# Twenty-four modulation vectors of layer 0: products on VectorE or on TensorE

## The chip, the core and the metric

The kernel runs on one NeuronCore of one Trainium2 chip. A core has engines that run side by side, each with its own instruction stream in program order: TensorE (PE, matrix products; its weight loads are shown apart as PEld), VectorE (DVE), ScalarE (ACT), GpSimd (POOL) and SyncE (SP), which here only starts DMA transfers. They wait for each other on semaphores. Data lie in SBUF (128 partitions) and PSUM (eight banks of 128 x 512 fp32, where TensorE writes). The metric is device microseconds (us) of one execution.

## The reference, cut to what matters

One step of a two-layer backbone over 1152 tokens (1024 latent, 128 context) of width 1024, with three token mixers (latent attention, mLSTM, HGRN2), an output projection and a SwiGLU feed-forward part. Each layer begins with modulation: six vectors of 1024 numbers for each of two conditions (`c` and `c_ctx`).

```python
def trunk_layer(x, cvec, lp, lb, cache, rope):
    mod = (jax.nn.silu(cvec) @ lp['w_mod'] + lp['b_mod'])[:, None, :]
    sh1, sc1, g1, sh2, sc2, g2 = jnp.split(mod, 6, axis=-1)
    h = x * (1 + sc1) + sh1
    ... h @ lp['w_in'], the three mixers, mix = concat @ lp['w_out']
    x = layernorm(ALPHA * x + g1 * mix, ...)
    h2 = x * (1 + sc2) + sh2
    ... feed-forward
    x = layernorm(ALPHA * x + g2 * (...), ...)
```

`w_mod` is 1024 x 6144 for each layer. In slices of 128 columns that is 48 products a layer, numbered j = 0 to 47: j 0 to 7 are `sh1`, 8 to 15 `sc1`, 16 to 23 `g1`, 24 to 31 `sh2`, 32 to 39 `sc2`, 40 to 47 `g2`. `sh1` and `sc1` are needed at once; `g1`, `sh2`, `sc2` only after the mixers.

## The kernel before, in words

The program goes layer by layer through phases A (input projections, HGRN2, preparation of the attention, mLSTM), B (attention), C (output projection) and D (feed-forward). Most products are fp32 split into a high and a low fp32r half and done as three matmuls (L155, L156, L157 in `mm3`); some, such as the mLSTM's, are plain fp32 matmuls, which the trace shows as two records each.

The modulation vectors sit in `modfm`, a tile with the 128 columns of a slice on the partitions and (j, condition) along the free axis. Those of layer 0 are made at three places: j 0 to 15 in the start stage (`start`, j 8 to 15 on TensorE at L251), j 40 to 47 later, and **j 16 to 39 in the background of other work**, by a generator `bg` that `start_mod` makes. At each `next(bg)` it does one j: a 512 KB transfer of the slice (L211, a ring of two buffers `raw`), and for each condition one VectorE instruction (L213) that multiplies 128 x 1024 weights by the condition, broadcast beforehand to all partitions (`cB`, L127, two transfers of 512 KB in each place), and accumulates the row sums into one column of `modfm`. Every eighth j adds the bias (`mod_bias`, L220). After j 23, `gsave` transposes the finished `g1` (L225) and stores it.

The generator is called at two places:

- zone "gemv" in phase A, j 16 to 23: once for each token tile n of the `gi` projection (evacuation L399), then for each tile of `ckv` and `cq` in `mla_prep`. These are long runs of `mm3` matmuls in PSUM banks 0 to 2 (`r_mm`), whose results VectorE takes out. In the same stretch VectorE prepares the gates of HGRN2 (L528 to L537).
- the mLSTM's output, `mlstm`, j 24 to 39: twice for each of nine token tiles n. For each n the scores of four heads (L830, into banks 3 and 4, `r_a`), the decay mask and exponential on POOL and ACT, the product with the scores on VectorE (L839), the state's part (L845, 128 x 130) and the values' part (L850, 128 x 65, both into banks 5 to 7, `r_m`), evacuations on VectorE (L846, L853) and the norm. Rows `snr` (L825) and queries `smq` (L826) are loaded for each n.

The order of instructions on each engine is not that of the code: the program is built with `schedule_with_timeline_sim=True`, and a list scheduler with its own model places them. So work of the next stage (rotations and query products of the attention, L1104 and L1134) stands among that of the mLSTM, and a change in one stage can shift the order in others. Each engine then keeps its order strictly. SP's queue too is in order: a transfer whose buffer isn't free yet holds up those behind it.

Layer 1 runs the same stages without `bg` (all its 48 vectors are made elsewhere), which makes it a comparison.

Of the kernel before, what the change touches and what calls it, by code (L numbers as in the profile page):

```python
# [20 lines left out]
P = 128  # L21
D = 1024
# [75 lines left out]
class Builder:  # L98
# [60 lines left out]
    def setup(self):  # L159
        nc, ctx, ins = self.nc, self.ctx, self.ins  # L160
        self.pp = self.pool(ctx, "persist")
        self.dram = self.pool(ctx, "scratch", bass.MemoryType.DRAM)
        self.pps = self.pool(ctx, "psum", bass.MemoryType.PSUM)
        t = self.tile
        self.bank = [t(self.pps, [P, 512], F32, "bank") for _ in range(8)]
        self.ident = t(self.pp, [P, P], name="ident")
        make_identity(nc, self.ident)
        self.hhi = t(self.pp, [P, KD, T], F32R, "hhi")
        self.hlo = t(self.pp, [P, KD, T], F32R, "hlo")
        self.cols = t(self.pp, [P, DEPTH, NCOL], name="cols")  # L170
        nc.sync.dma_start(self.cols, ins["cols"])
        self.modfm = t(self.pp, [P, DEPTH, 48, 2], name="modfm")
        self.gates = t(self.pp, [P, NT, 16], name="gates")
        self.gT = t(self.pp, [16, P], name="gT")
        self.mhalf = t(self.pp, [P, 8], name="mhalf")
        nc.vector.memset(self.mhalf, -0.5)
        lbt = t(self.pp, [P, 12], name="lbt")
        lb0 = self.cols[:, 0, COL_OFF["lb"][0]:COL_OFF["lb"][0] + 4].rearrange("p (a d) -> p a d", d=2)
        L = lbt.rearrange("p (a b) -> p a b", b=6)
        nc.vector.tensor_tensor(L[:, :, 0:1], lb0[:, :, 0:1], lb0[:, :, 1:2], op=ALU.max)  # L180
        nc.vector.tensor_tensor(L[:, :, 1:3], lb0, L[:, :, 0:1].to_broadcast([P, 2, 2]), op=ALU.subtract)
        nc.scalar.activation(L[:, :, 1:3], L[:, :, 1:3], AF.Exp)
        nc.vector.tensor_tensor(L[:, :, 3:4], L[:, :, 1:2], L[:, :, 2:3], op=ALU.add)
        nc.vector.reciprocal(L[:, :, 3:4], L[:, :, 3:4])
        nc.vector.tensor_tensor(L[:, :, 1:3], L[:, :, 1:3], L[:, :, 3:4].to_broadcast([P, 2, 2]), op=ALU.mult)
        self.lbL = L
        dr = self.dram
        self.s_x = t(dr, [T, D], name="sx")
        self.s_x2 = t(dr, [T, D], name="sx2")
        self.s_tm = {k: t(dr, [T, 256], name="s" + k) for k in ("mo", "gg")}  # L190
        self.s_cq = t(dr, [P, 2, T], name="scq")
        self.s_ck = t(dr, [P, T], name="sck")
        self.s_kp = t(dr, [32, T], name="skp")
        self.s_mq = t(dr, [P, 2, T], name="smq")
        self.s_rec = t(dr, [T, 512], name="srec")
        self.s_c = t(dr, [2, D], name="scr")
        self.s_g = {g: t(dr, [16, P], name="sg") for g in (16, 40)}
        self.s_nr = t(dr, [8, T], name="snr")
        self.s_ri = [t(dr, [1, 512], name="sri") for _ in range(4)]
        self.s_dn = [t(dr, [1, 512], name="sdn") for _ in range(4)]  # L200
        self.s_ws = t(dr, [8, T], name="sws")
        self.s_ex = [t(dr, [P, 4, T2], name="sex") for _ in range(3)]
        self.s_h = [[t(dr, [NT, P, b - a, P], name="shid") for a, b in ps] for ps in PASSES]
# [31 lines left out]
    def start(self, z):  # L235
        nc, ins = self.nc, self.ins
        accs = [(i // NB, i % NB, self.bank[i]) for i in range(7)]
        cin, cc = z([P, KD, 2]), z([P, KD, 2])
        cB, junk = [z([P, D]), z([P, D])], z([P, D], BF16)
        rm, rx, rt = z.ring(6, [P, U]), z.ring(6, [P, T]), z.ring(2, [P, T])  # L240
        nc.sync.dma_start(cin, ins["cvec"])
        nc.scalar.activation(cc, cin, AF.Silu)
        bm = self.col(0, "bmod")
        xs, ws = [], []

        def mods(k):
            v, j = rm.next(), 8 + k
            nc.sync.dma_start(v, ins["w_mod"][0, j])
            ps = self.bank[7][:, 2 * j:2 * j + 2]
            for i in range(KD):  # L250
                nc.tensor.matmul(ps, v[:, i * P:(i + 1) * P], cc[:, i, :], start=(i == 0), stop=(i == KD - 1))  # L251
            nc.vector.tensor_scalar(self.modfm[:, 0, j, :], ps, bm[:, j:j + 1], 1.0, op0=ALU.add, op1=ALU.add)
            if k == 0:
                self.mod_init(cB, ins["crow"])
                for s in range(2):
                    nc.scalar.activation(cB[s], cB[s], AF.Silu)
                    nc.sync.dma_start(self.s_c[s:s + 1, :], cB[s][0:1, :])
            self.mod_gemv(0, k, cB, rm.next(), junk)
            self.mod_bias(0, k, 1)
            xs.append(rx.next())  # L260
            nc.sync.dma_start(xs[k], ins["xT"][:, k, :])

        mods(0)
        for k in range(KD):
            if k < 3:
                ws.append(self.unit(ins["w_in"][0, k]))
            if k + 1 < KD:
                mods(k + 1)
            x2 = rt.next()
            for s, c in ((0, slice(0, NLAT)), (1, slice(NLAT, T))):  # L270
                if s == 0:
                    nc.scalar.activation(x2[:, c], xs[k][:, c], AF.Identity, bias=self.modfm[:, 0, k, s:s + 1], scale=self.modfm[:, 0, 8 + k, s:s + 1])
                else:
                    nc.vector.tensor_scalar(x2[:, c], xs[k][:, c], self.modfm[:, 0, 8 + k, s:s + 1], self.modfm[:, 0, k, s:s + 1], op0=ALU.mult, op1=ALU.add)
            self.split(self.hhi[:, k, :], self.hlo[:, k, :], x2, nc.vector if k % 2 else nc.gpsimd)
            for u, b, ps in accs:
                if u < len(ws):
                    for kk in (range(k + 1) if u == k else (k,)):
                        self.fm_step(ps, ws[u], kk, b)
        return ws, accs  # L280

    def start_mod(self, z, j0, j1):
        raw = z.ring(2, [P, U])
        cB, junk = [z([P, D]), z([P, D])], z([P, D], BF16)
        self.mod_init(cB)

        def gen():
            for j in range(j0, j1):
                self.mod_gemv(0, j, cB, raw.next(), junk)
                if j % 8 == 7:  # L290
                    self.mod_bias(0, j - 7, 8)
                if j == 23:
                    self.gsave(0, 16, self.r_m.next())
                yield

        return gen()

# [69 lines left out]
    def phase_a(self, l):  # L367
# [5 lines left out]
        with ExitStack() as cA:  # L373
# [10 lines left out]
            with ExitStack() as cH:  # L384
# [4 lines left out]
                with ExitStack() as c0:  # L389
                    zs = Zone(self, c0, f"hs{l}", "right")  # L390
                    set0 = [zs([P, T]) for _ in range(5)]
                    self.mark(f"hg{l}")
                    g.project(0, set0, early if l == 0 else None)
                    self.row(l, "b_gi", br)
                    with ExitStack() as c:
                        bg = self.start_mod(Zone(self, c, "gemv"), 16, 24) if l == 0 else iter(())

                        def gi(ps, tt):
                            V.tensor_tensor(v[:, tt, :], ps, br, op=ALU.add)  # L399
                            next(bg, None)  # L400

                        self.win_tm(l, "gi", gi)
                        g.prep(0, set0, rW)
                        self.mark(f"mp{l}")
                        self.mla_prep(l, Zone(self, c, f"mp{l}"), bg, (brx, nr))
                    self.mark(f"hs{l}")
                    zt = Zone(self, cH, f"ht{l}")
                    set1 = [zt([P, T]) for _ in range(5)]
                    g.states(0, set0, v, rW)
                    for b in range(NB):  # L410
                        g.outs(0, b, set0, v, rW)
                        g.project_unit(1, b, set1)
# [28 lines left out]
            self.mark(f"ml{l}")  # L441
            with ExitStack() as c:
                zl = Zone(self, c, f"ml{l}")
                bg = self.start_mod(zl, 24, 40) if l == 0 else iter(())
                self.mlstm(l, gates, vaug, mkT, Cst, zl, bg)
                for i in tail:
                    fill[int(i)]()
# [1242 lines left out]
def pack(i):  # L1690
# [8 lines left out]
    a["w_mod"] = np.concatenate([  # L1699
        wm[0, :, :, :8].transpose(2, 3, 0, 1).reshape(8, P, 1024),  # L1700
        wm[0, :, :, 8:16].transpose(2, 1, 0, 3).reshape(8, P, 1024),
        wm[0, :, :, 16:].transpose(2, 3, 0, 1).reshape(32, P, 1024),
        wm[1].transpose(2, 3, 0, 1).reshape(48, P, 1024)], 0).reshape(DEPTH, 48, P, 1024)
    w = f["w_in"].reshape(DEPTH, KD, P, -1)
    units = np.zeros((DEPTH, 22, P, 1024), np.float32)
# [63 lines left out]
```

## Time and profile before

| quantity | value |
|---|---|
| median of three runs | 3624.28 us (3616.66 to 3624.41) |
| profiled execution | 3608.53 us, span 3606.7 us |
| PE busy | 3382.4 us (94%) |
| DVE busy | 2251.9 us (62%) |
| ACT, POOL busy | 1635.2 us (45%), 1999.0 us (55%) |
| mean granted TensorE clock | 0.952 |

The span is the time from the first to the last instruction in the profiled execution; what lies around it is 1.8 us. Busy is the time in which at least one instruction of the engine ran. The granted clock is the share of 2.4 GHz that TensorE had: 1.00 or 0.50 at any moment, and a mean over a stretch. Matmuls are pipelined, so the spacing of starts says what one costs, not its duration.

### The profile page before, as it was taken

To read this page: it belongs to the slowest core of one execution; us is meant where nothing else is said; L and a number is where in the kernel's file an instruction comes from. 1 tells how busy PE (TensorE), PEld (TensorE's weight loads), DVE (VectorE), ACT (ScalarE), POOL (GpSimd) and SP (SyncE) were. 2 spreads that over 40 slices of the span, in tenths; PEclk is the share of its full clock that TensorE was granted. 3 is DMA by queue.
4 is the path that set the end of the run, shared out by engine and by line. 5 is a ranking of instruction groups with operands and counts; after the bars stand their busy time and mean duration, and the time that the engine had idled before them with its cause. 6 is when DMAs were issued, how large, how long until landed. Compare 5 with 4: busy or idle time off the path is not lost. (4 is left out here: it accounts for less than half of the span.)

```text
span 3606.7 us, 56103 instructions
## 1 busy us (share of the span) xinstructions
PE 3382.4 (94%) x20556; PEld 3015.5 (84%) x20556; DVE 2251.9 (62%) x4487; ACT 1635.2 (45%) x2877; POOL 1999.0 (55%) x1750
## 2 busy tenths in 40 slices
PE   7998987998979999999889989989999899999989
PEld 7998876776779999988689888877767899999867
DVE  6878778556674444487776688765568544443344
ACT  4264654887343333312262646578863433333111
POOL 3465566877665555401454556457763555556345
PEclk9999976999989999999999999789999899999999
DMA  6211153002352222375422021401044322224232
GB/s 251 70 46 34 45 168 98 19 21 85 123 156 86 85 86 86 104 252 184 161 73 71 32 43 40 135 25 24 22 129 127 115 76 75 75 77 158 72 116 77
DMA packets 331274, 335.77 MB, mean 93 GB/s; under 512 B 191459, under 2 KB 270387, under 8 KB 330997
## 3 DMA queue, kind: packets, MB, share of 16 engines
q1 hardware_dynamic: 330996, 332.19, 29.3%
q8 instruction: 161, 2.64, 0.3%
q14 instruction: 117, 0.95, 0.1%
HBM read 263.54 MB, written 68.56 MB: 92 GB/s over the span
## 5 line engine op out<-in xcount | busy, mean ns | idle before, releaser
L151 POOL TENSOR_TENSOR t<-t,t 128x512 fp32r<-128x512 f32 (+3 forms) x318 | 440.5, 1387 | 384.9 <-ACT t L150 379.9
L1447 PE MATMUL bank<-hhi,t 128*128 128x256 f32 (+1 forms) x2816 | 571.2, 295 | 7.9 <-DVE t L1347 7.4
L150 ACT CAST t<-t 128x512 fp32r<-128x512 f32 (+5 forms) x404 | 270.5, 672 | 676.1 <-PE bank L1447 275.1
L155 PE MATMUL bank<-hhi,t 128*128 128x384 f32 (+1 forms) x1238 | 464.3, 381 | 24.8 <-ACT hhi L145 10.4
L157 PE MATMUL bank<-hhi,t 128*128 128x384 f32 (+1 forms) x1238 | 463.8, 376 | 5.8 <-DVE t L151 5.8
L156 PE MATMUL bank<-hlo,t 128*128 128x384 f32 (+1 forms) x1238 | 464.4, 375 | 4.6 <-POOL hlo L151 3.1
L1447 PEld LDWEIGHTS bank<-hhi,t 128*128 128x128 f32 x2816 | 456.4, 189 | 9.6 <-ACT t L150 7.4
L1185 POOL TENSOR_TENSOR t<-t,t 128x512 fp32r<-128x512 f32 (+1 forms) x304 | 384.2, 1283 | 123.4 <-ACT t L1184 107.4
L1447 PE MATMUL bank<-t,t 128*128 128x320 f32 (+1 forms) x3168 | 435.0, 297 | 4.6 <-ACT t L150 2.2
L1447 PEld LDWEIGHTS bank<-t,t 128*128 128x128 f32 x3168 | 428.2, 190 | 6.0 <-ACT t L150 3.0
L1447 PE MATMUL bank<-hlo,t 128*128 128x320 f32 (+1 forms) x1408 | 415.3, 295 | 0.1
L155 PE MATMUL bank<-t,hhi 128*128 128x256 f32 (+3 forms) x1232 | 387.1, 315 | 8.1 <-DVE t L1105 2.1
L156 PE MATMUL bank<-t,hhi 128*128 128x256 f32 (+3 forms) x1232 | 389.2, 316 | 4.9 <-POOL t L146 4.9
L157 PE MATMUL bank<-t,hlo 128*128 128x256 f32 (+3 forms) x1232 | 388.9, 316 | 0.1
L155 PEld LDWEIGHTS bank<-hhi,t 128*128 128x128 f32 x1238 | 241.4, 196 | 60.7 <-ACT hhi L145 11.3
L1135 DVE TENSOR_REDUCE t<-bank 128x1 f32<-128x384 f32 (+1 forms) x400 | 205.1, 539 | 129.9 <-PE bank L1134 127.5
L157 PEld LDWEIGHTS bank<-hhi,t 128*128 128x128 f32 x1238 | 240.9, 195 | 37.9 <-DVE t L151 9.0
L156 PEld LDWEIGHTS bank<-hlo,t 128*128 128x128 f32 x1238 | 241.3, 195 | 36.7 <-POOL hlo L151 3.9
L1447 PEld LDWEIGHTS bank<-hlo,t 128*128 128x128 f32 x1408 | 265.4, 189 | 0.4 <-issue 0.2
L213 DVE SCALAR_TENSOR_TENSOR t<-t,t 128x1024 bf16<-128x1024 f32 x176 | 239.4, 1360 | 36.0 <-DMA t<-in_w_mod_dram 29.0
L155 PEld LDWEIGHTS bank<-t,hhi 128*128 128x128 f32 x1232 | 240.4, 196 | 24.9 <-DVE t L1105 2.5
L156 PEld LDWEIGHTS bank<-t,hhi 128*128 128x128 f32 x1232 | 241.7, 196 | 21.1 <-POOL t L146 5.3
(355 smaller groups left out, 7250.6 us busy)
## 6 DMA issues: line engine op xcount, KB each, us to landing
t<-in_w_mod_dram SPq DMA_DIRECT2D x96, 512.0 KB
t<-in_w_ffn_in_dram SPq DMA_DIRECT2D x88, 512.0 KB
t<-in_w_ffn_out_dram SPq DMA_DIRECT2D x44, 512.0 KB
t<-in_w_in_dram SPq DMA_DIRECT2D x40, 512.0 KB
shid<-t SPq DMA_DIRECT2D x88, 160.0 KB
sx<-t SPq DMA_DIRECT2D x27, 512.0 KB
t<-sx SPq DMA_DIRECT2D x27, 512.0 KB
shid<-t SPq DMA_DIRECT2D x88, 128.0 KB
```

The source lines that it names most:

```text
L150: self.nc.scalar.copy(hi, src)
L151: (eng or self.nc.gpsimd).tensor_tensor(lo, src, hi.bitcast(F32), op=ALU.subtract)
L155: mm(ps, a[0], b[0], start=first, stop=False)
L156: mm(ps, a[0], b[1], start=False, stop=False)
L157: mm(ps, a[1], b[0], start=False, stop=last)
L213: nc.vector.scalar_tensor_tensor(junk, raw, 1.0, cB[s], op0=ALU.mult, op1=ALU.mult, accum_out=self.modfm[:, l, j, s:s + 1])
L1135: V.tensor_reduce(nm[:, i, b:b + 1] if i < 8 else nm[:, i, 3:4], ps, axis=AX.X, op=ALU.max, negate=True)
L1185: G.tensor_tensor(pl, e, ph.bitcast(F32), op=ALU.subtract)
L1447: mm(ps, a[x][:, k * P:(k + 1) * P], view(y, k, n0, n1), start=first and k == 0 and i == 0, stop=k == 3 and i == 2, skip_group_check=True)
```

## The change

For j 16 to 39 of layer 0 the product is done on TensorE. `start_mod` now works in groups of four j. A group starts four transfers of 512 KB into a ring of four buffers (L291), then yields `gap` times (9 in the first place, 4 in the mLSTM), then issues eight fp32 matmuls (L296) with the condition `cc` (128 x 2, a tile that now stays for good) as the stationary side and 128 x 512 weights as the moving side, accumulating 2 x 512 numbers in one bank. ACT copies them to SBUF (L298), four transposes (L301) bring them to the partitions, and one VectorE instruction (L304) adds the bias and writes `modfm` for four j. The bank of the matmuls comes from `r_m` (5 to 7) in the first place and from `r_a` (3, 4) in the mLSTM. There are two groups in the first place and four in the mLSTM. The broadcasts `cB`, the 48 VectorE products and the three bias additions go. The host lays the 24 slices of `w_mod` out in the new order. Lines behind L306 of before are 13 further down in the changed kernel (L830 is L843, L845 is L858, L850 is L863).

```diff
+        self.cc = t(self.pp, [P, KD, 2], name="cc")
...
-        cin, cc = z([P, KD, 2]), z([P, KD, 2])
+        cin, cc = z([P, KD, 2]), self.cc
...
-    def start_mod(self, z, j0, j1):
-        raw = z.ring(2, [P, U])
-        cB, junk = [z([P, D]), z([P, D])], z([P, D], BF16)
-        self.mod_init(cB)
+    def start_mod(self, z, j0, j1, r_ps, gap):
+        nc = self.nc
+        raw, row = z.ring(4, [P, U]), z.ring(1, [2, 512])

         def gen():
-            for j in range(j0, j1):
-                self.mod_gemv(0, j, cB, raw.next(), junk)
-                if j % 8 == 7:
-                    self.mod_bias(0, j - 7, 8)
-                if j == 23:
+            for j in range(j0, j1, 4):
+                ws = [raw.next() for _ in range(4)]
+                for u, w in enumerate(ws):
+                    nc.sync.dma_start(w, self.ins["w_mod"][0, j + u])
+                for _ in range(gap):
+                    yield
+                ps, r = r_ps.next(), row.next()
+                for k in range(KD):
+                    nc.tensor.matmul(ps[0:2, :], self.cc[:, k, :], ws[k // 2][:, (k % 2) * 512:(k % 2 + 1) * 512],
+                                     start=(k == 0), stop=(k == KD - 1))
+                nc.scalar.copy(r, ps[0:2, :])
+                ps = self.r_m.next()
+                for q in range(4):
+                    nc.tensor.transpose(ps[:, 2 * q:2 * q + 2], r[:, q * P:(q + 1) * P], self.ident[0:2, 0:2])
+                one = 1.0 if (j // 8) % 3 == 1 else 0.0
+                b = self.col(0, "bmod")[:, j:j + 4].unsqueeze(2).to_broadcast([P, 4, 2])
+                nc.vector.scalar_tensor_tensor(self.modfm[:, 0, j:j + 4, :], ps[:, 0:8].rearrange("p (j s) -> p j s", s=2), one, b,
+                                               op0=ALU.add, op1=ALU.add)
+                if j == 20:
                     self.gsave(0, 16, self.r_m.next())
-                yield
...
-                        bg = self.start_mod(Zone(self, c, "gemv"), 16, 24) if l == 0 else iter(())
+                        bg = self.start_mod(Zone(self, c, "gemv"), 16, 24, self.r_m, 9) if l == 0 else iter(())
...
-                bg = self.start_mod(zl, 24, 40) if l == 0 else iter(())
+                bg = self.start_mod(zl, 24, 40, self.r_a, 4) if l == 0 else iter(())
...
-        wm[0, :, :, 16:].transpose(2, 3, 0, 1).reshape(32, P, 1024),
+        wm[0, :, :, 16:40].reshape(4, 2, P, 6, 4, P).transpose(3, 0, 2, 1, 4, 5).reshape(24, P, 1024),
+        wm[0, :, :, 40:].transpose(2, 3, 0, 1).reshape(8, P, 1024),
```

How the order moves. On VectorE, in the first place, before (`t_835` is the discarded product, L399 the evacuation of `gi`):

```order
L528 TENSOR_SCALAR t_635<-t_744,t_721,t_717 128x384
L399 TENSOR_TENSOR t_619<-bank_64,t_166 128x256 [waits PE_49]
L213 SCALAR_TENSOR_TENSOR t_835,modfm_80<-t_819,t_827 128x1024 [waits DMAHW5_49,DVE_49]
L530 TENSOR_SCALAR t_631<-t_627 128x384 [waits DVE_49]
L533 SCALAR_TENSOR_TENSOR t_639<-t_623,t_639 128x384 [waits Activation_49]
L529 TENSOR_SCALAR t_635<-t_635 128x384 [waits DVE_49]
L399 TENSOR_TENSOR t_619<-bank_65,t_166 128x256 [waits PE_49]
L213 SCALAR_TENSOR_TENSOR t_835,modfm_80<-t_819,t_831 128x1024 [waits DVE_49]
```

and in the changed kernel at the same place (L412 is L399 of before, L541 to L550 are L528 to L537):

```order
L541 TENSOR_SCALAR t_619<-t_744,t_717,t_713 128x384
L546 SCALAR_TENSOR_TENSOR t_623<-t_627,t_623 128x384 [waits Activation_49]
L412 TENSOR_TENSOR t_615<-bank_63,t_167 128x256 [waits PE_49]
L543 TENSOR_SCALAR t_635<-t_631 128x384 [waits DVE_49]
L542 TENSOR_SCALAR t_619<-t_619 128x384 [waits DVE_49]
L550 SCALAR_TENSOR_TENSOR t_744<-t_645,t_623 128x384 [waits DVE_49]
L544 SCALAR_TENSOR_TENSOR t_631<-t_635,t_631 128x384 [waits DVE_49]
L412 TENSOR_TENSOR t_615<-bank_64,t_167 128x256 [waits PE_49]
```

The long products are gone from between the gate preparation and the evacuations.

On TensorE, among the tiles of the `mLSTM`, before (`bank_66` and `bank_67` are banks 3 and 4, `bank_68` to `bank_70` are 5 to 7):

```order
L850 MATMUL bank_70<-t_611,t_4374 128x65 x2
L830 MATMUL bank_67<-t_4394,t_615 128x128 [waits DVE_49]
L830 MATMUL bank_67<-t_4394,t_615 128x128
L845 MATMUL bank_68<-t_2986,t_4390 128x130 [waits DVE_49]
L845 MATMUL bank_68<-t_2986,t_4390 128x130
L830 MATMUL bank_66<-t_4386,t_615 128x128 [waits DMAHW6_49,DVE_49]
```

and in the changed kernel (`t_4353`, `t_4357`, `t_4361` and `t_4365` are the four weight buffers, `cc_81` the condition):

```order
L863 MATMUL bank_69<-t_607,t_4381 128x65 [waits DMAHW7_49,DVE_49,Pool_49]
L296 MATMUL bank_66<-t_4353,cc_81 2x512 [waits DMAHW7_49,DVE_49]
L296 MATMUL bank_66<-t_4353,cc_81 2x512
L296 MATMUL bank_66<-t_4357,cc_81 2x512 [waits DMAHW0_49]
L296 MATMUL bank_66<-t_4357,cc_81 2x512
L296 MATMUL bank_66<-t_4361,cc_81 2x512 [waits DMAHW1_49]
L296 MATMUL bank_66<-t_4361,cc_81 2x512
L296 MATMUL bank_66<-t_4365,cc_81 2x512 [waits DMAHW1_49]
L296 MATMUL bank_66<-t_4365,cc_81 2x512
L863 MATMUL bank_69<-t_607,t_4381 128x65 [waits DVE_49]
L863 MATMUL bank_69<-t_607,t_4381 128x65 x2
```

A group stands as one block between two matmuls of the same values' part, in a bank of the scores, and each pair of its matmuls waits for its own transfer.

On SP, in the same stage of the changed kernel (L838 and L839 are L825 and L826 of before, L1034 the loads for the attention, L888 a store of the mLSTM's result):

```order
L291 DMA t_4353<-in_w_mod_dram 128x1024 [waits DMAHW1_49,PE_49]
L1034 DMA t_5700<-skp_99 32x384 [waits DMAHW3_49,DMAHW2_49,DVE_49]
L291 DMA t_4357<-in_w_mod_dram 128x1024 [waits PE_49]
L1034 DMA t_5688<-scq_97 128x384 [waits DMAHW4_49,DVE_49]
L1034 DMA t_5692<-scq_97 128x384 [waits DMAHW6_49,DMAHW5_49,DVE_49]
L291 DMA t_4361<-in_w_mod_dram 128x1024 [waits PE_49]
L888 DMA srec_101<-t_4421 128x256 [waits DMAHW7_49,Pool_49]
L352 DMA sgg_96<-t_163 128x256 [waits DMAHW0_49,Pool_49]
L291 DMA t_4365<-in_w_mod_dram 128x1024 [waits DMAHW1_49,PE_49]
L1034 DMA t_5696<-scq_97 128x384 [waits DMAHW2_49,DVE_49]
L839 DMA t_4397<-smq_100 128x2x128 [waits DMAHW3_49,PE_49]
L838 DMA t_4381<-snr_105 128x8x128 [waits DMAHW4_49,PE_49]
```

The transfers of the second group wait (`PE_49`) until the first group's matmuls have read the buffers, and the loads of queries and rows for the mLSTM's tiles stand behind them; before, the transfers of L211 stood singly among the same loads and waited for VectorE.

## Rows read from the trace of the kernel before

**Rows 1.** The page: span, busy time by engine, granted clock in 40 slices.

```profile
span 3606.7 us, 56103 instructions
PE 3382.4 (94%) x20556; PEld 3015.5 (84%) x20556; DVE 2251.9 (62%) x4487; ACT 1635.2 (45%) x2877; POOL 1999.0 (55%) x1750
...
PEclk9999976999989999999999999789999899999999
```

**Rows 2.** Line L213 on VectorE: durations in ns, minimum, median, maximum.

```profile
L213 DVE SCALAR_TENSOR_TENSOR t<-t,t x176: 1161/1224/3507, 10.5 to 1751.6; 128x1024 bf16<-128x1024 f32 x176
L213 DVE DVE_READ_ACCUMULATOR t<-t,t x176: 71/80/89, 11.6 to 1752.8; 128x1 f32 x176
```

**Rows 3.** Windows, L213 alone: us, DVE busy, clock, DMA share, GB/s.

```profile
69.00:130.00 61.00, 22.22 (x32) 0.89 0.31 103
469.90:613.90 144.00, 42.95 (x64) 0.62 0.46 149
```

**Rows 4.** Windows by stage: length, then busy PE, PEld, DVE, ACT, POOL, clock.

```profile
91.70:191.40 99.70, 94.38 (x744) 92.04 (x743) 85.78 (x256) 29.82 (x44) 48.46 (x50) 0.93 0.24 73
1900.80:1983.10 82.30, 82.30 (x705) 81.02 (x704) 50.70 (x202) 15.07 (x25) 30.98 (x35) 1.00 0.23 68
469.90:613.90 144.00, 105.79 (x466) 90.22 (x465) 125.34 (x337) 59.57 (x136) 98.00 (x98) 0.62 0.46 149
2263.30:2385.50 122.20, 104.21 (x495) 91.06 (x495) 97.94 (x308) 66.15 (x156) 57.80 (x68) 0.65 0.36 108
77.30:91.70 14.40, 8.91 (x46) 8.19 (x45) 14.40 (x23) 4.86 (x6) 6.52 (x4) 0.67 0.45 150
1887.90:1900.80 12.90, 9.30 (x62) 8.70 (x61) 10.79 (x12) 12.09 (x16) 8.82 (x7) 0.87 0.27 94
```

**Rows 5.** Waits of PE: 469.9 to 613.9 (two), then 69 to 192.

```profile
PE bank L830 <- DMA t<-smq: 10.1, 3, 4.7
PE bank L1134 <- DVE t L1135: 8.3, 7, 3.4
...
PE bank L225 <- DVE modfm L220: 3.5, 1, 3.5
```

**Rows 6.** Waits of SP's queue, 469.9 to 613.9: us in total, times, longest.

```profile
SPq L211 <- DVE t L860: 6.6, 2, 5.2
...
SPq L211 <- DVE t L213: 4.3, 2, 2.9
```

**Rows 7.** Timeline of PE: start, us, instructions; four short stretches.

```profile
55.43 1.84 PE L251 MATMUL bank<-t,t 128*128 128x2 f32 x16
...
400.70 0.71 PE L791 MATMUL bank<-t,t 128*128 128x130 f32 x4
401.25 0.38 PE L781 MATMUL bank<-ident,t 128*128 128x128 f32 x2
...
493.31 1.61 PE L845 MATMUL bank<-t,t 128*128 128x130 f32 x6
...
613.17 0.39 PE L1180 MATMUL bank<-t,t 96*128 96x512 f32 x1
613.40 0.39 PE L1181 MATMUL bank<-t,t 96*128 96x512 f32 x1
```

**Rows 8.** ACT copies by form: busy us, mean ns, idle before.

```profile
L1196 ACT COPY t<-bank 1x512 f32<-1x512 f32 x32 | 18.6, 580 | 4.5 <-PE bank L1255 3.7
```

**Rows 9.** Windows within the stages, columns as in rows 4.

```profile
30.80:68.00 37.20, 34.49 (x223) 33.41 (x223) 23.74 (x48) 17.47 (x18) 11.26 (x4) 1.00 0.60 227
494.00:505.00 11.00, 10.00 (x48) 8.60 (x46) 9.82 (x28) 6.55 (x17) 4.01 (x5) 0.50 0.67 221
2296.00:2305.00 9.00, 9.00 (x47) 8.20 (x47) 7.87 (x27) 4.93 (x15) 3.48 (x5) 0.50 0.61 186
```

## The prediction

> **What bounds the kernel now.** I read the page first. TensorE is busy 94% of the span, so over the whole kernel it is the bound, and VectorE at 62% is not [rows 1]. That mean hides the two places that the change touches. The row of the granted clock has its deepest dip in slices 5 and 6, 451 to 631 us: the second place, the mLSTM. [...] The first place lies in slices 0 to 2, at 9.
>
> Next the line that goes. L213 has a median of 1224 ns and an accumulator read of 80 ns behind it [rows 2]. Its windows give the busy time by place: 22.2 us in the first (32 records are 16 products and 16 reads), 42.95 us in the mLSTM [rows 3]. So 65.2 us of VectorE work go.
>
> What these are worth is read from each stage, with layer 1, which has no such work, as the comparison [rows 4]. First place, evacuation of `gi` to the end of `cq`: 99.7 us with 744 matmuls in layer 0, 82.3 us with 705 in layer 1, and there TensorE is busy all of the 82.3 us at clock 1.00; layer 0 has it busy 94.4 of 99.7 us at 0.93. mLSTM's output, from its first scores to the attention's first values product: 144.0 us in layer 0, 122.2 us in layer 1. VectorE is busy 125.3 of the 144 us and TensorE only 105.8, at 0.62. So VectorE is near the bound in both stages, by chains: it evacuates late, and TensorE waits for the bank or the operand.
>
> Last the waits. In the mLSTM's stage TensorE's longest sum is on a transfer, L830 for `smq`, 10.1 us in three waits, then 8.3 us for a reduction in the attention's part; in the first place L225 waits 3.5 us for the bias line L220, the end of the L213 chain [rows 5]. SP itself waits for VectorE at L211, 6.6 and 4.3 us [rows 6], with the loads of `smq` queued behind it: one way in which L213 costs time without standing on TensorE's path.
>
> **The change, part by part.**
>
> *A group on TensorE.* The trace has no fp32 matmul with 512 moving columns, so I bound it. Below: fp32 shows two records for each matmul, and a record of 512 fp32r columns starts 0.23 us after the one before it at full clock (613.17 to 613.40), so 0.46 us. Above: four records, two fp32 matmuls, of 130 columns take 0.55 us (400.70 to 401.25), 0.275 us each; scaled with the columns, 512/130 of it is 1.08 us [rows 7]. The upper row also holds a load of 128 stationary columns, of which two are left here, so I take less than the upper end, 0.9 us. Eight matmuls are 7.2 us (3.7 to 8.7). The four transposes have two moving columns like L251, 16 records or eight matmuls in 1.84 us: 0.23 us each, 0.9 us [rows 7]. A group is 8.1 us (4.6 to 9.6) at full clock. At 1.2 GHz it is twice that, 16.2 us: the six records of L845 at 493.31 take 1.61 us, 0.27 us each, where those of 130 columns above took 0.14 us.
>
> *First place.* Two groups add 16.2 us (9 to 19). What goes: at layer 1's rate 744 matmuls would take 744/705 x 82.3 = 86.9 us, 12.8 us less; the lead-in of the stage takes 14.4 us against 12.9, 1.5 us; the 3.5 us wait of L225 becomes a wait for L304, which I leave at a third. The gain is at most 12.8 + 1.5 + 3.5 = 17.8 us, and 0 if layer 0 is slow there for other reasons (its ACT and POOL have more to do too, 29.8 and 48.5 us against 15.1 and 31.0). VectorE's 85.8 of 99.7 us speaks for most of it: I take 15. TensorE would be full, so the groups stand on the path: 16.2 - 15 = +1 (9 - 18 = -9 to +19).
>
> *mLSTM.* Four groups add 32.4 us (18 to 38). Relief: 144.0 - 122.2 = 21.8 us at most, by layer 1; 0 at least. POOL is busy 98 us here against 58 in layer 1, still far from 144, so I take 18. Without L213 the stage would be 126 us with TensorE busy 106: of the 20 idle us the groups, which depend on nothing but their transfers, can fill half, -10; bounds 0 and -20. The clock: a group runs without a pause, and work behind it may start at 2.4 GHz that now runs at 1.2; if that lasts as long as the group's own 8 us, 16 us of slow work becomes 8 us, over four groups 32 us at most, 0 at least. I take 8, a quarter, as most of the matmuls behind are short ones with waits. Sum: 32.4 - 18 - 10 - 8 = -4. All the good ends together would be 18 - 22 - 20 - 32, which can't be had at once since the idle is filled only once: I hold -25. The bad end is 38.
>
> *ACT and VectorE's own additions.* Six copies like L1196, 0.58 us each [rows 8], and six small VectorE instructions. Nothing is queued behind them but other stages' work with slack; 0, at most 3.5 us. *Transfers:* four broadcasts of 512 KB go, the 24 slices stay; 0. *Order of phases A and B:* the scheduler shifts rows as far as the attention; with no term to name I take 0, and -4 to +4 for the range.
>
> *Sum.* +1 - 4 = -3 us, on 3608.5 us of the profiled execution: 3605.5. That execution lies 15.8 us below the median of the runs. On the median's scale it is 3621, rounded to 3620.
>
> **What the clock does in a group.** Two stretches speak against the groups running at full clock: in the mLSTM of layer 0 TensorE is busy 10.0 of 11 us and the granted clock is 0.50, the level of 1.2 GHz; in layer 1, 9.0 of 9 us and 0.50. The work there is the mLSTM's fp32 matmuls. In the start stage, with the projections' matmuls and some L251, 34.5 of 37.2 us busy go with 1.00 [rows 9]. Which level the groups get, no row shows. [...]
>
> **Rivals.**
>
> 1. *The clock stays at 1.2 GHz in the mLSTM's groups.* Place: the four blocks of eight matmuls. Then they cost 4 x 16.2 = 65 us; less 18 for VectorE, less 10 for idle time, +37, with the first place +1: 3624 + 38 = 3662. For it: the 0.50 rows [rows 9] and 0.62 over the stage. Against: the groups wait for nothing once their weights are there, like the start stage's long runs at 1.00, and the first place has 0.93 already. It decides from about 1.5 us for one L296. Chance 0.17.
> 2. *The weights come late.* The ring holds one group, so a group's transfers start when the one before has been read, and 2 MB go in about 14 us at the stage's 149 GB/s [rows 3]. If a group's first matmul stands earlier in TensorE's order, TensorE stops there, and all mLSTM work behind it with it; on SP the queries' loads stand behind transfers that wait for TensorE, like those that now cost L830 10.1 us [rows 5]. At 5 us a group in six groups it is 30 us less the 10 that I let idle time hide: -3 + 20 = +17, 3641. Against: the stage is long, some 20 us between two groups at half clock. Chance 0.13.
> 3. *VectorE's relief pays in full and the groups hide.* Both stages become as fast as layer 1's (17.8 and 21.8 us gained), the mLSTM's groups fit into the 38 us in which TensorE is idle there now, and only the first place's 16 us stand on the path: 16 - 18 - 22 = -24, 3600. For it: VectorE at 125 of 144 us. Against: idle time is by chains, and a block of 7 us put before a short matmul delays what waits for it. Chance 0.30.
> 4. *Hidden anyway.* VectorE's products fill gaps between other waits, and the groups fill TensorE's: nothing moves, 3624. It lies in the forecast's own range.
>
> **How the numbers follow.** The forecast and the fourth rival together have 0.40, at 3609 to 3632, so 3620 with its own range. 0.3%, about 11 us, is what a measurement of this kernel can tell from no change. Faster by more: the third rival and a little of the forecast's lower edge, 0.33. Within: 0.38. Slower by more: the first two and the upper edge, 0.29. The range reaches from the third rival's time, 3598, to where the second ends and the first begins, 3650, leaving about 0.08 below and 0.12 above.
>
> **What the changed profile would show.** L296 starting every 0.9 us, and the clock in its blocks: 1.00, or 0.50 with 1.8 us. VectorE's busy time down by 65 us to about 2187. The first place's stage (L412 to the last of `cq`) 100 us long with TensorE full; the mLSTM's stage about 140 us with VectorE near 82. TensorE's wait for L296's transfers under 2 us a group; a larger one is the second rival. The prediction is wrong if the mLSTM's stage falls to about 122 us or rises above 160, or if a stage that the change doesn't touch (the feed-forward part, layer 1) moves by more than 4 us.

## The result and the profile after

The changed kernel takes 3592.43 us (median of four runs, 3583.56 to 3593.66), the kernel before 3620.72 us (four runs, 3616.66 to 3624.41): a ratio of 0.9918, 95% interval 0.99 to 0.9936. It is 0.8% faster. The forecast was 3620 us with a range of 3598 to 3650, so the time lies below the range.

The page of the changed kernel, to be read beside [rows 1]:

```profile
span 3590.6 us, 56270 instructions
PE 3397.8 (95%) x20676; PEld 3001.4 (84%) x20676; DVE 2188.8 (61%) x4394; ACT 1639.1 (46%) x2883; POOL 1980.5 (55%) x1750
...
PEclk9999988999989999999999999789999999999999
```

VectorE lost 63 us, and TensorE gained only 15 us of busy time though it was given some 45 us of matmuls: its other work got shorter, and the clock's dip in slices 5 and 6 (counted from 0) went from 7 and 6 tenths to 8 and 8.

The stages, as windows of the changed kernel (length, busy PE, PEld, DVE, ACT, POOL, clock, DMA share, GB/s): the first place, the mLSTM's tiles up to the last values product, the attention's lead from there to its first values product, and both together. They answer to [rows 4].

```profile
87.30:189.70 102.40, 99.71 (x742) 86.06 (x743) 65.25 (x225) 27.35 (x42) 37.08 (x41) 1.00 0.25 75
...
468.30:552.00 83.70, 77.37 (x399) 48.89 (x399) 50.12 (x193) 36.12 (x86) 49.74 (x71) 0.90 0.62 199
552.00:599.40 47.40, 39.60 (x162) 30.36 (x162) 34.09 (x83) 26.75 (x54) 24.55 (x28) 0.71 0.22 68
...
468.30:599.40 131.10, 116.97 (x559) 79.25 (x559) 84.21 (x276) 62.87 (x140) 74.29 (x98) 0.83 0.48 152
```

The same two parts of the mLSTM's stage before:

```profile
469.90:552.30 82.40, 62.64 (x324) 56.50 (x322) 69.64 (x209) 33.03 (x84) 55.91 (x61) 0.65 0.55 177
552.30:613.90 61.60, 43.15 (x144) 33.72 (x144) 55.69 (x129) 26.54 (x52) 42.10 (x37) 0.58 0.34 111
```

The tiles, where the four groups stand (the end of the last one reaches into the lead), are 1.3 us longer; the lead behind them is 14.2 us shorter. There, before, VectorE was busy 55.7 of 61.6 us, 16.9 us of it with products left over from the generator (window of before, L213 alone: VectorE busy, records, clock, DMA share, GB/s), in front of the evacuations that the attention waits for. Now it is busy 34.1 of 47.4 us.

```profile
552.30:613.90 61.60, 16.94 (x26) 0.58 0.34 111
```

TensorE's waits in the lead (us in total, times, longest) say the same. Before it waited 8.3 us for VectorE's reductions L1135 [rows 5] and 5.0 us for L1105; after, with these lines renamed L1148 and L1118, 3.1 and 1.2 us:

```profile
PE bank L155 <- DVE t L1105: 5.0, 3, 2.1
```

```profile
PE bank L1147 <- DVE t L1148: 3.1, 5, 1.2
PE bank L155 <- DVE t L1118: 1.2, 1, 1.2
```

The stretch ahead of the first place changed too. The last 14.4 us before the first evacuation of `gi` had VectorE busy throughout and TensorE busy for 8.9 us at clock 0.67 [rows 4]; in the changed kernel the same length has

```profile
72.90:87.30 14.40, 13.85 (x98) 12.57 (x96) 12.91 (x21) 12.10 (x16) 9.70 (x9) 1.00 0.28 88
```

and the evacuation begins 4.4 us earlier, at 87.3 instead of 91.7 us.

The groups themselves, TensorE's timeline (start, us, instructions; 16 records are eight matmuls):

```profile
146.73 7.03 PE L296 MATMUL bank<-t,cc 128*2 128x512 f32 x16 [0.59 <-ACT t L950]
...
484.56 7.03 PE L296 MATMUL bank<-t,cc 128*2 128x512 f32 x16
508.69 7.75 PE L296 MATMUL bank<-t,cc 128*2 128x512 f32 x12
...
524.29 0.41 PE L301 MATMUL bank<-ident,t 2*128 2x2 f32 x4
525.85 7.03 PE L296 MATMUL bank<-t,cc 128*2 128x512 f32 x16
```

7.03 us for eight is 0.88 us each, where 0.9 was forecast; four transposes take 0.41 us, not 0.9. One group, at 508.69, began at clock 0.50: its first records start 0.81 to 0.86 us apart, where the others start 0.43 us apart. Of TensorE's waits in the tiles only one is the change's own, and none is for the weights:

```profile
PE bank L301 <- ACT t L298: 4.6, 1, 4.6
PE bank L843 <- DMA t<-smq: 1.4, 1, 1.4
```

The wait of L830 (now L843) for `smq`, 10.1 us in [rows 5], is 1.4 us now.

### The profile page after: what moved, and what is told of

The parts are those of the page before. It is cut to its first block, busy times and chain, and to the rows that moved or that the text cites. A ratio compares the mean times of both kernels' runs of the same rounds, so it can differ in the third digit from the quotient of the medians.

```text
span 3590.6 us, 56270 instructions
## 1 busy us (share of the span) xinstructions
PE 3397.8 (95%) x20676; PEld 3001.4 (84%) x20676; DVE 2188.8 (61%) x4394; ACT 1639.1 (46%) x2883; POOL 1980.5 (55%) x1750
## 5 line engine op out<-in xcount | busy, mean ns | idle before, releaser
L1148 DVE TENSOR_REDUCE t<-bank 128x1 f32<-128x384 f32 (+1 forms) x400 | 205.3, 539 | 125.8 <-PE bank L1147 123.5
L157 PEld LDWEIGHTS bank<-t,hlo 128*128 128x128 f32 x1232 | 238.0, 193 | 15.4 <-POOL hlo L151 0.8
```

The source lines that it names most:

```text
L157: mm(ps, a[1], b[0], start=False, stop=last)
L1148: V.tensor_reduce(nm[:, i, b:b + 1] if i < 8 else nm[:, i, 3:4], ps, axis=AX.X, op=ALU.max, negate=True)
```

## The experiments

**Which place pays.** Each place alone, the other as before (cut; the comments are added here).

```diff
-                bg = self.start_mod(zl, 24, 40, self.r_a, 4) if l == 0 else iter(())
+                bg = self.start_mod_v(zl, 24, 40) if l == 0 else iter(())      # e1: old generator here
...
-  self.start_mod(Zone(self, c, "gemv"), 16, 24, self.r_m, 9)
+  self.start_mod_v(Zone(self, c, "gemv"), 16, 24)                              # e2: old generator here
```

> The vectors j 16 to 23 go to TensorE, j 24 to 39 stay on VectorE as before. Theory A (the gain lies in the mLSTM's stage and the attention's lead behind it): the first place is worth 2 to 5 us, so 3616 to 3619 on before's median of 3621. Theory B (VectorE's relief in the first place pays as much as that in the mLSTM): 3606 to 3610.

Measured 3610.6 us against 3614.8 for the kernel before beside it, ratio 0.9985 (0.9972 to 0.9999).

> The vectors j 24 to 39 go to TensorE, j 16 to 23 stay on VectorE as before. Theory A: nearly the whole gain, 3595 to 3600, with the stretch from the mLSTM's last values product to the attention's first (61.6 us before, 47.4 after) at 47 to 50 us. Theory B: about half, 3606 to 3610.

Measured 3595.3 us against the same 3614.8, ratio 0.9939 (0.9917 to 0.9961); the lead took 45.3 us. Theory A holds: the mLSTM's place carries about 20 us, the first about 4.

e2's trace shows something more. It has the same code in the mLSTM as the changed kernel, in another order. Its tiles and its whole stage, as windows, are

```profile
471.80:546.20 74.40, 72.38 (x400) 44.31 (x399) 49.31 (x191) 34.09 (x85) 51.30 (x74) 1.00 0.69 228
471.80:591.20 119.40, 107.95 (x544) 73.15 (x544) 84.73 (x275) 59.59 (x136) 74.15 (x97) 0.89 0.52 170
```

The clock never falls in the tiles, and the stage is 11.7 us shorter than the changed kernel's 131.1. So one trace fixes what this stage takes only to some 10 us. (The traced execution took 3587.2 us, the fastest of e2's six.)

**What a group costs and what the relief is worth.** In e3 (its edit follows) the groups stay, but seven of eight matmuls have 16 columns; in e4 the old kernel keeps its products and gets the matmuls of the groups on top, without their copies and transposes.

```diff
+                    n = 512 if k == 0 else 16
-                    nc.tensor.matmul(ps[0:2, :], self.cc[:, k, :], ws[k // 2][:, (k % 2) * 512:(k % 2 + 1) * 512],
+                    nc.tensor.matmul(ps[0:2, 0:n], self.cc[:, k, :], ws[k // 2][:, (k % 2) * 512:(k % 2) * 512 + n],
```

> As the changed kernel, but seven of the eight matmuls of each group take 16 columns instead of 512 (the vectors are not computed fully); transfers, waits and order stay. Theory C (a group raises the granted clock and so pays for itself): taking 6 x 5.4 = 32 us of TensorE work away gains under 8 us, 3584 to 3596, and the clock in the mLSTM's tiles falls back from about 0.88 to 0.6 to 0.7. Theory D (a group costs what it takes, VectorE's relief pays for it): 25 to 32 us faster than the changed kernel, 3560 to 3568.

> As before, with VectorE's products, and six groups of eight 2 x 512 fp32 matmuls added whose result nobody reads. Theory C: the clock in the mLSTM's tiles rises from about 0.63 to 0.8 or more and pays for most of the 7 us of a group there; with two groups of the first place on the path the time is 3620 to 3636. Theory D: all 42 us stand on the path less what idle time hides, 3645 to 3663.

e3 takes 3571.1 us, ratio 0.9873 (0.9842 to 0.9905): 21 us less than the changed kernel. e4 takes 3636.9, ratio 1.0053 (1.0034 to 1.0072): 22 us more than before beside it. e3 lies nearer to D. e4's time is at the upper edge of C, but both ranges were counted from 3621 for the kernel before, and beside e4 that took 3614.8; as differences, C said -1 to +15 and D +24 to +42, so e4 too lies between them and nearer to D. Half of the added 42 us shows. e3's stages, as windows (tiles, lead, both, first place):

```profile
454.00:517.70 63.70, 59.53 (x396) 50.18 (x396) 43.21 (x169) 35.19 (x85) 40.12 (x59) 0.84 0.75 250
517.70:569.40 51.70, 42.11 (x179) 33.56 (x179) 44.21 (x108) 29.45 (x60) 34.19 (x41) 0.70 0.28 82
454.00:569.40 115.40, 101.64 (x573) 83.74 (x573) 87.42 (x276) 64.65 (x145) 74.32 (x99) 0.78 0.54 175
87.70:179.40 91.70, 88.66 (x740) 84.67 (x741) 63.95 (x224) 26.81 (x42) 37.27 (x40) 1.00 0.27 84
```

Without VectorE's products, and with groups of about 1.7 us (7.03 less 5.3, an estimate; in the first place TensorE is busy 88.66 us in e3 and 99.71 in the changed kernel, 5.5 us less a group), the mLSTM's stage is 115.4 us: 28.6 us below before. The long groups then add 15.7 us (13.0 by the second trace of the changed kernel, below), for the 4 x 5.3 = 21 us of matmuls that e3 takes out: two thirds or so stand on the path there. By e2's trace it is only 4.0 us. The order did not stay as the expectation had it: the scheduler split e3's groups and moved work of the attention (179 matmul records in the lead, where the changed kernel has 162), so the two numbers hold the shift of order as well. And e3's traced execution, 3564.1 us, was 7 us under its median, so the 28.6 us may be some us too much. The medians, with the first place in them, point the same way: e3 is 43.7 us below before beside it, and the changed kernel 21.3 us above e3. In the first place they add 102.4 - 91.7 = 10.7 us for 2 x 5.3: all of it. The clock in e3's tiles is 0.84, against 0.65 before, without any long group, and taking the long groups away made the kernel faster: theory C, that a group pays for itself, falls. But the groups raise the clock as well, by single traces. In e4, with the groups and the products, it is 0.76 over the stage, against 0.62 before [rows 4], and in e2, with long groups and no products, 1.00 in the tiles and 0.89 over the stage. How much of the clock each of the two brings was not separated. e4's tiles take 121.1 us; its scheduler finished the products there, and the lead behind is 42.6 us instead of 61.6. That fits what the leftovers cost in the lead. The whole stage of e4, with products and groups, is

```profile
476.70:640.40 163.70, 132.00 (x560) 87.69 (x559) 127.01 (x339) 63.30 (x142) 88.13 (x99) 0.76 0.41 129
```

which is 32.6 us above the changed kernel's, with groups in both.

**Does the profiled run of before stand for before?** A second trace of the unchanged kernel.

> The kernel before, unchanged, for a second trace of it. If the runs of before differ (3608 to 3630 us) because the granted clock dips at other moments, the stretches with the mLSTM's and the attention's small matmuls differ in length by 3 to 8 us each from the first trace, at another clock, and the feed-forward part by less than 3 us. If they differ by something outside the two changed places, these agree within 2 us with the first trace (144 and 102 us).

That execution took 3618.3 us, 9.8 us more than the first. The mLSTM's stage and the first place agree with the first trace within 1.2 us (145.1 and 99.9 us, where the first trace had 144.0 and 99.7; the 102 us of the expectation is the changed kernel's), the feed-forward part too; the difference is 4.8 us in the start stage and 6.5 us in the attention. The start stage's two executions, windows of the first trace and then of the second (columns as above):

```profile
48.00:60.00 12.00, 12.00 (x88) 12.00 (x87) 9.71 (x26) 4.79 (x4) 2.97 (x2) 1.00 0.12 30
60.00:72.00 12.00, 10.56 (x59) 9.81 (x59) 5.61 (x7) 9.30 (x15) 4.21 (x2) 1.00 0.50 171
```

```profile
48.00:60.00 12.00, 12.00 (x66) 12.00 (x65) 5.93 (x15) 2.41 (x3) 2.44 (x1) 0.72 0.02 5
60.00:72.00 12.00, 12.00 (x56) 12.00 (x56) 7.71 (x16) 6.50 (x6) 3.25 (x1) 0.72 0.44 128
```

The same program, the clock 1.00 in one and 0.72 in the other. The expectation had looked for it in the mLSTM; it is elsewhere. Of the other traces e4's alone has this dip, and why is open. A second dip goes with the products: in all five traces with VectorE's products in the first place, or e9's reductions (before, e2, e4, e5, e9), the clock is 0.50 for 3.4 to 10.2 us shortly before `gi` or as it begins, and `gi` begins at 88.3 to 96.5 us; in all nine with the new first place it stays at 1.00 there, and `gi` begins at 86.2 to 87.7 us. So part of the start stage's difference belongs to the change.

**The wait for ACT's copy.** In e6 the transposes of a group come two yields later (cut; the comment is added here); e8 is the changed kernel again.

```diff
+                for i in range(gap):
+                    yield
+                    if i == 1 and late is not None:
+                        finish(*late)      # transposes and bias of the group before
+                        late = None
```

> As the changed kernel, but the four transposes of a group come two yields later. Theory E (TensorE's wait of 4.6 us for ACT's copy in the mLSTM, and the half clock from 500 to 515 us behind it, are a cost of where the transposes stand): the mLSTM's tiles take 72 to 78 us instead of 83.7, 3580 to 3587 in all. Theory F (the dip comes by chance): the same as the changed kernel within 5 us, 3588 to 3597.

> The changed kernel again, beside the others on the same chip. Theory E: the wait for ACT's copy at the first group (4.6 us) and the half clock behind it are there again, the mLSTM's tiles take 82 to 86 us. Theory F: the dip is elsewhere or absent, and the tiles take 74 to 80 us in a trace with the same order of instructions.

e6: 3596.9 us, ratio 0.9934 (0.9914 to 0.9953); e8: 3589.5 us, ratio 0.9913 (0.9896 to 0.9931). In e8's trace the same wait, in the same order of instructions, is

```profile
PE bank L843 <- DMA t<-smq: 1.7, 2, 1.5
PE bank L301 <- ACT t L298: 0.4, 1, 0.4
```

and the tiles take 82.0 us instead of 83.7. The clock from 500 to 515 us is 0.66 there and 0.55 in the first trace, so the dip came again without the wait. In e6 the tiles take 95.8 us, with the clock at 0.50 from 480 to 490 us. Theory E falls: the wait isn't what makes the dip, and late transposes bring nothing. The 4.6 us came by chance and cost 2 us at most. Theory F had the tiles at 74 to 80 us in e8 and missed that too; what makes the dip is open.

**Shorter groups.** In e7 the mLSTM's groups run as fp32r, through ACT copies of the weights (cut).

```diff
+                    if j0 > 16:
+                        wr, cr = rr.next(), ccr
+                        nc.scalar.copy(wr, ws[k // 2][:, (k % 2) * 512:(k % 2 + 1) * 512])
+                    nc.tensor.matmul(ps[0:2, :], cr[:, k, :], wr,
```

> As the changed kernel, but in the mLSTM the weights go through ACT copies to fp32r and the 32 matmuls run as fp32r, with the rounding that this brings. If a group's cost on TensorE is what is left to gain (four groups are 20 us longer than the short ones there), about 4 x 5.2 = 21 us less of TensorE work brings 12 to 20 us: 3573 to 3581, unless ACT's 32 copies of about 0.6 us (19 us) delay the exponentials; then 3588 to 3600.

3581.2 us (3578 to 3586; e8 beside it 3587 to 3593), ratio 0.9891 (0.9871 to 0.9912): the fastest whole version here, with 16 of the vectors made by fp32r products. It is 8 us below the changed kernel beside it, short of the 12 to 20 us expected. The tiles take 75.6 us, with ACT busy 57 us instead of 36.

**Does VectorE slow GpSimd?** GpSimd's groups in the mLSTM's stage by form (busy us, mean ns), before and after (cut), are the same instructions:

```profile
L874 POOL TENSOR_TENSOR t<-t,t 128x256 f32<-128x256 f32 x18 | 17.6, 981 | 0.9 <-DVE t L869 0.5
L863 POOL TENSOR_TENSOR t<-t,t 128x256 f32<-128x256 f32 x18 | 15.1, 856 | 3.5 <-DVE t L860 3.4
...
L864 POOL TENSOR_TENSOR t<-t 128x256 f32<-128x256 f32 x9 | 11.8, 1309 | 0.3
```

```profile
L887 POOL TENSOR_TENSOR t<-t,t 128x256 f32<-128x256 f32 x18 | 12.7, 711 | 5.5 <-DVE t L882 4.3 <-DVE t L873 0.8
L876 POOL TENSOR_TENSOR t<-t,t 128x256 f32<-128x256 f32 x18 | 11.2, 643 | 8.9 <-DVE t L873 8.8
...
L877 POOL TENSOR_TENSOR t<-t 128x256 f32<-128x256 f32 x9 | 7.5, 831 | 0.2
```

The 98 us of GpSimd in [rows 4] became 74 with the same 98 instructions. Was that the relief? e9 replaces the old products by reductions with one input; e11 and e12 put 32 VectorE instructions back into the changed kernel's mLSTM, with two inputs (45 us in all) and with one (38 us). The edits, cut, with comments added:

```diff
-                self.mod_gemv(0, j, cB, raw.next(), junk)                                         # e9, on before
+                    self.nc.vector.tensor_reduce(self.modfm[:, 0, j, s:s + 1], w, axis=AX.X, op=ALU.max)
...
+  nc.vector.scalar_tensor_tensor(junk, ws[u], 1.0, ws[3 - u], ..., accum_out=acc[:, s:s + 1])    # e11, on after
+  nc.vector.tensor_reduce(acc[:, s:s + 1], ws[u], axis=AX.X, op=ALU.max)                         # e12, on after
```

> As before, but each of the 48 VectorE products of the two places is a reduction over the same 128 x 1024 weights alone (one input from SBUF instead of two; the vectors come out as something else). VectorE's load stays, about 1.1 to 1.3 us each. Theory G (the products slow GpSimd, whose instructions with the same shapes were 0.86, 0.98 and 1.31 us beside them and 0.64, 0.71 and 0.83 us without): these fall to 0.65, 0.72 and 0.85 us, GpSimd's busy time in the mLSTM's stage from 98 to about 76 us, and the stage from 144 to 128 to 136 us; 3600 to 3610. Theory H (VectorE's own time is what costs): GpSimd stays near 95 us or falls without effect, the stage stays at 141 to 147 us, 3614 to 3624.

> The changed kernel, and in the mLSTM 32 VectorE products of two weight buffers each (128 x 1024, two SBUF inputs, the form of the old products; nobody reads the sums). Theory G: GpSimd's instructions are back at 0.85 to 1.3 us, its busy time in the stage from 74 to 90 us or more, and the kernel is 12 to 25 us slower than the changed one, 3603 to 3616, and 8 us or more slower than with one input. Theory H: 15 to 25 us slower, as with one input within 4 us.

> The changed kernel, and in the mLSTM 32 VectorE reductions of one weight buffer each (128 x 1024, one SBUF input, 1.2 us each, nobody reads them). Theory G: GpSimd stays at 74 to 78 us in the stage, and with VectorE busy about 123 us the kernel is 4 to 12 us slower than the changed one, 3595 to 3603. Theory H: 15 to 25 us slower, 3606 to 3616.

e9: 3596.3 us, ratio 0.9944 (0.9923 to 0.9965). e11: 3626.5, ratio 1.0029 (1.0015 to 1.0043). e12: 3622.5, ratio 1.001 (0.9995 to 1.0024). e11 and e12 are 34 and 30 us above the changed kernel's median, more than either theory had. GpSimd in e11 and then in e12:

```profile
L881 POOL TENSOR_TENSOR t<-t,t 128x256 f32<-128x256 f32 x18 | 15.1, 858 | 8.3 <-DVE t L878 8.1
```

```profile
L881 POOL TENSOR_TENSOR t<-t,t 128x256 f32<-128x256 f32 x18 | 11.0, 636 | 9.8 <-DVE t L878 7.3 <-DVE t L876 2.3
```

and the mLSTM's stage of each, from its first scores as before:

```profile
472.50:622.80 150.30, 128.34 (x522) 87.11 (x523) 124.77 (x325) 58.85 (x130) 89.43 (x95) 0.74 0.41 131
```

```profile
472.40:622.70 150.30, 123.16 (x522) 81.97 (x523) 118.38 (x293) 58.75 (x130) 71.27 (x95) 0.74 0.42 131
```

The slowing of GpSimd is real and follows the second input: 0.86 us in before and in e11, with two inputs, against 0.64 us in the changed kernel, 0.64 in e12 and 0.67 in e9, with one input or none. Why the second input does it, no run shows. But it doesn't set the stage: 150.3 us both ways, with GpSimd at 89 or 71 us. There theory H holds, though not its size: VectorE's own time and place in the queue cost 19 to 22 us of stage (against 131.1 and 128.4 us in the two traces of the changed kernel), and 3 to 5 us more go ahead of it, where TensorE waits 3.1 us for `smq` before the first scores. On before the pair is less clear. e9's mLSTM stage is 140.8 us, 3.2 less than before, though GpSimd's busy time in it fell from 98 to 73 us: there it is H, falling without effect. Yet the kernel gains 21 us, which neither theory had, and 10 of them lie between the two places, where no product stood (268.1 us instead of 278.5). Whether that is the moved order or GpSimd was not settled. (The traced execution of e9 was its fastest, 3587.6 us against a median of 3596.3.)

**Is GpSimd late now?** e10 moves its scaling and normalisation to VectorE.

```diff
-        LG = V if l else G
+        LG = V
```

> As the changed kernel, but in layer 0 too the mLSTM's scaling and normalisation (36 instructions of 0.64 to 0.71 us on GpSimd) run on VectorE, as in layer 1. If GpSimd is now late in the tiles, its 24 us go and VectorE pays 36 x 0.42 = 15 us: the mLSTM's tiles take 76 to 80 us instead of 82 to 84, 3583 to 3590. If TensorE is the bound there, nothing: 3588 to 3597.

3592.3 us, ratio 0.9927 (0.9911 to 0.9943): nothing, as expected if TensorE is the bound.

## Why the prediction was wrong

- *What failed is the relief in the mLSTM:* "21.8 us at most, by layer 1 ... I take 18". e3 measures 28.6 us and e4 against the changed kernel 32.6, both above the bound, by single traces in their own orders. The difference to a sister stage was read as a limit. Layer 1's stage has its own VectorE load, 98 us of 122 [rows 4], and its length is no fixed number either: 116.0 to 122.6 us over fourteen traces. 32 reductions of 1.2 us put back (e12) cost 19 to 22 us, 0.5 to 0.6 us for each us of VectorE, and by e3 it is 0.67; I had counted 0.4. So the term was too small by every experiment, and by how much depends on the order. Much of what the products delayed was not in the tiles but in the lead behind them, where leftovers stood before the attention's evacuations.
- *The other terms of that stage held as a sum.* Four groups less what idle time and the clock give back were 32.4 - 10 - 8 = 14.4 us; the traces of the changed kernel put 15.7 and 13.0 us above e3, e2's 4.0. The split between idle time and clock was not measured, and no run shows the 8 us of the clock by themselves: the clock rose from 0.62 to 0.83 over the stage, and to 0.78 in e3 with short groups, so most of the rise needs no long group.
- *The stage in all:* -4 forecast, -12.9 measured (28.6 won, 15.7 given back); -15.6 by e8's trace, -24.6 by e2's. The third rival's size for the kernel (-24) was near the result, but its story only in part: in the changed kernel's own traces the groups don't hide, and the gain is in the lead.
- *First place: the sum nearly held,* +1 forecast and -1.7 measured, by terms that were off both ways. e3's trace ends the place 12.0 us earlier, where 15 of relief were taken, with some 3.4 us of short groups in it; the long ones put 10.7 us back, all on the path. The lead-in was put at 1.5 us by layer 1; it became 4.4 us shorter. From `gi` to `cq` the place itself is 2.7 us longer.
- *The price of a group was nearly right:* 0.88 us for 0.9 a matmul, 0.41 us for 0.9 the transposes. So was the clock that the sum took: 1.00 in all records of five groups, and 0.50 in the first six of the sixteen records of the one at 508.69. What decides the level was not shown. A busy TensorE alone doesn't bring 1.00: between two groups it is busy for 8 of 8 us at 0.50 (the window of all engines, in the changed kernel):

```profile
500.00:508.00 8.00, 8.00 (x34) 7.09 (x33) 4.22 (x14) 3.27 (x8) 6.58 (x10) 0.50 0.68 227
```

- *Rivals.* The first, with 1.8 us for one L296, fell, though part of one group ran near that level: its first records, two to a matmul, start 0.81 to 0.86 us apart. The second fell too: no wait for the weights.
- *The scale.* I took the profiled execution as 15.8 us below before's median and carried that over to the changed kernel. Its own profiled execution stands at its median. Profile against profile the change is -16.2 us, medians differ by 28; the first trace of before was one of its fastest (3608 to 3632 us over all its executions). Of the miss of 28 us, 9 are the mLSTM's term, 4 the other stages together, and 15 this shift. Not all of it is chance. From the second trace of before, which is nearer its median, the change is -26.0 us: -14.0 in the mLSTM's stage, -9.2 in the start stage, -7.7 in the attention, +4.9 in the rest. The start stage was taken as untouched but for its lead-in, and its second dip goes with the old products; how much of the rest is due to the change stays open. Layer 1's mLSTM, which the prediction named as a sign of being wrong, is 5.9 us shorter in the first trace of the changed kernel than in the first of before, inside its spread over the fourteen traces.

## What to carry to other kernels

Work that leaves a queue is worth what waits behind it, and that can be in the stage after: here the leftovers of a background generator stood before the next stage's evacuations. A sister stage without the work is an estimate, not a bound; the short-group trick of e3 (keep the transfers, cut the columns) tells relief and cost apart, as far as the scheduler's order and the one trace allow. The work queued for a place can also slow the stage ahead of it. Before a forecast below 0.5%, look whether the one trace is a typical execution.

## What the runs showed of the hardware

- A fp32 matmul of 512 columns on two stationary columns takes 0.88 us at clock 1.00 (7.03 us for eight, in the changed kernel); the weight load of one record takes 0.08 us against 0.19 us for 128 columns (minimum, median and maximum in ns, after the colon).

```profile
L296 PEld LDWEIGHTS bank<-t,cc x96: 80/85/129, 78.5 to 553.1; 128*2 128x2 f32 x96
L863 PEld LDWEIGHTS bank<-t,t x144: 186/192/337, 472.4 to 552.0; 128*128 128x128 f32 x144
```

- The trace gives the granted clock as a share of full speed, 1.00 or 0.50. The 1.2 and 2.4 GHz of the prediction are an estimate for these two levels: in before, records of 128 x 384 at 0.50 start 0.32 us apart, 1.2 columns per ns, if a column takes a cycle. Half the clock is about twice the time: at 1.00 the same records start 0.17 us apart, and those of L296 0.43 us, against 0.81 to 0.86 at 0.50.
- The same GpSimd instructions of 128 x 256 (L863 of before) take 0.64 us without two-input VectorE products beside them (changed kernel and e12) and 0.86 us with them (before and e11), a third more.
- The same program has its clock at 1.00 or 0.72 in the same 24 us of the start stage in two executions (before and e5), and the start stage is 4.8 us longer in the second.
